# A chunked delta-rule kernel: each level of the triangular inverse forms D and its transpose from one product, and q S leaves PSUM chunk by chunk

## The chip, the cores and the metric

The kernel runs on 1 core of one Trainium2 chip. The metric is the device time of one execution in microseconds (us). Three runs of the kernel before gave 1337.87, 1337.9 and 1339.18 us, so its median is 1337.9 us. The profiled execution is a run of its own.

## The reference, cut to what matters

A decoder trunk of two layers works on 528 tokens (16 meta tokens and 512 others) of width 1024. Layer 0 mixes tokens with a gated delta rule in 8 heads of dimension 128, layer 1 with a short convolution. A gated ConvFFN and a layer norm follow each. The change lies in the delta rule, which the reference writes like this for each head, chunk by chunk:

```
m = where(strict, einsum("id,jd->ij", k_beta, k) * decay, 0)
a_mat = eye(CHUNK) + m
u = triangular_solve(a_mat, v_beta)
w = triangular_solve(a_mat, k_beta * exp(g))
...
v_new = u_i - w_i @ state
o_i = qg_i @ state + qk_i @ v_new
state = state * exp(gl_i) + kd_i.T @ v_new
```

The rest of the trunk is projections by large weight matrices, a width-3 convolution, gating and layer norms.

## The kernel before, in words

**The large products.** Each float32 operand is split into a high part and a rest (`split`, L88 on ACT and L89 on DVE), and each product is three matmuls (L272, L273, L274). Weights come as strips of 128 x 128 blocks: SP loads a strip (L199), ACT and DVE split it, PE uses it.

**The delta-rule stage** is the `with ExitStack() as gctx` block, L313 to L668. It uses 5 chunks of 106 positions (`NC_`, `CH`). It has these parts for each head `hd`:

- `proj` (L392): the q, k and v projections, 144 matmuls into tiles `ps`, with copies to SBUF by ACT (L410, L411), a convolution on DVE (L415) and a Silu on ACT (L417).
- `gdn_a` (L440): transposes and products of k, v and q (tiles `pk`, `pv`, `pn`, `pp`, `pq`, `psNb`), then the inverse of the unit triangular matrix, then one refinement in higher precision (`pr`, `pz`, `py`, L523 to L545), which leaves `DT`.
- `gdn_b` (L548): the recurrence over the 5 chunks. In a chunk, PE multiplies the state `St` by k (L560, `sa[0]`) and by q (L561, `sb`), DVE forms `rr` (L562), PE multiplies by the inverse (L565, `sa[1]`), ACT forms `vn` (L566), PE forms the update (L569, `sa[2]`) and DVE the new `St` (L573). After the last chunk DVE scales all of `sb` into `oS` (L575), PE forms the part within the chunks (L579, L582), and the output is normalised: DVE adds (L580), ACT squares (L589), DVE and POOL form the factor (L591, L592, L593), DVE scales (L594).
- `gdn_c` (L598): PE transposes `oS` (L604, tile `pot`) and ACT copies it into `h` (L607, L608).
- `gate` (L611): the z projection, 48 matmuls into `psz`, a Silu on ACT (L618). When all is done, `h` is multiplied by `zs` (L665), split into `hh` and `hl` (L667), which hold the input of the z projection until then, and POOL issues a DMA that reloads the residual (L668).

**The inverse before** (L497 to L521) has 7 levels, for blocks of 1, 2, 4 up to 64. After level 0, a level is: PE forms p1 from `N16` and `D16` (L502); ACT copies it to `T16` (L507); PE forms p2 from `DT16` and `T16` (L513); DVE copies p2 into `D16` where the level's mask is set (L514); PE transposes `D16` (L518, tile `pt`); ACT copies it to `DT16` (L519). The five chunks are five matmuls of 106 x 106 in float16 in each step. Each of p1, p2 and pt is a new tile of the same PSUM slot (`gtile`, tag `ga0` for even heads, `ga1` for odd ones, one buffer).

**The order of the work.** The generators of a stage are woven (`weave`, L627): while head `hd` is in `gdn_b`, head `hd+1` does the second part of `gdn_a`, head `hd+2` the first `AH` pieces of it, and head `hd-1` its `gdn_c`, after `CW` empty turns. The program order gives priorities; the framework's scheduler then fixes one order for each engine, and takes later work, a `ps` or `psz` matmul above all, where it expects earlier work not to be ready. So `ps` and `psz` are the filler of this stage. After it the first product of the rest of the kernel is `pd` (`down`, L745).

Of the kernel before, what the change touches and what calls it, by code (L numbers as in the profile page):

```python
# [73 lines left out]
def tile_hybrid_trunk(ctx, tc, xt, par, cst, msk, w_ba, w_qkv, w_z, w_ao, w_bi, w_bo, w_up, w_dn, out):  # L74
# [21 lines left out]
    msk_sb = cpool.tile([P, len(LEVELS), CH], U8, name="msk_sb")  # L96
# [216 lines left out]
    with ExitStack() as gctx:  # L313
# [6 lines left out]
        for l0 in (0, NC_):  # L320
            l1 = min(l0 + NC_, len(LEVELS))
            mskf = gp.tile([P, NC_, CH], F32, name=f"mskf{l0}", tag="B", bufs=2)
            nc.sync.dma_start(mskf[:, : l1 - l0, :], msk[:, l0:l1, :])
            V.tensor_copy(msk_sb[:, l0:l1, :], mskf[:, : l1 - l0, :])
# [115 lines left out]
        def gdn_a(hd, box, qT, kT, vT, PT):  # L440
# [7 lines left out]
            NT, DT = full("NT"), full("DT", 3)  # L448
            kd = gp.tile([CH, NC_, P], F32, name=f"kd{hd}", tag="kd", bufs=3)
# [22 lines left out]
            G.tensor_copy(D16, bcm(ident16[:CH, :CH], NC_))  # L472
            yield 900, 1200
# [20 lines left out]
            V.tensor_scalar(N16, NT, NSC, None, ALU.mult)  # L494
            yield 900, 2200

            for li in range(len(LEVELS)):  # L497
                m_d = bcm(msk_sb[:CH, li, :], NC_)
                p1 = gtile(f"p1{hd}{li}", ch)
                for c in R5:  # L500
                    r_ = D16[:, c, :] if li else ident_dn[:CH, :CH]
                    TE.matmul(p1[:CH, c, :CH], N16[:, c, :], r_, start=True, stop=True)  # L502
                last = li == len(LEVELS) - 1
                if li == 0:
                    V.copy_predicated(D16, m_d, p1[:CH, :NC_, :CH])
                else:
                    S.activation(T16, p1[:CH, :NC_, :CH], AF.Copy, scale=1.0 / NSC)  # L507
                    if li == 1:
                        V.scalar_tensor_tensor(L16, NT, NSC, N16, ALU.mult, ALU.subtract)
                    yield 250, 1500  # L510
                    p2 = gtile(f"p2{hd}{li}", ch)
                    for c in R5:
                        TE.matmul(p2[:CH, c, :CH], DT16[:, c, :], T16[:, c, :], start=True, stop=True)  # L513
                    V.copy_predicated(D16, m_d, p2[:CH, :NC_, :CH])  # L514
                yield 250, 1500
                pt = gtile(f"pt{hd}{li}", ch, F16)
                for c in R5:
                    TE.transpose(pt[:CH, c, :CH], D16[:, c, :], ident16[:CH, :CH])  # L518
                S.activation(DT16, pt[:CH, :NC_, :CH], AF.Copy)  # L519
                if not last:  # L520
                    yield 250, 1500  # L521
# [26 lines left out]
        def gdn_b(hd, box):  # L548
# [7 lines left out]
            sb = gbank(f"sb{hd}", "gc")  # L556
            for c in R5:
                r_ = vb[:, c, :]
                if c > 0:
                    TE.matmul(sa[:CH, 0, :], kTv[:, c, :], St, start=True, stop=True)  # L560
                    TE.matmul(sb[:CH, c - 1, :], qTv[:, c, :], St, start=True, stop=True)  # L561
# [5 lines left out]
                yield 220, 800  # L567
                if c < NC_ - 1:
# [6 lines left out]
            V.tensor_tensor(oS[:, 1:, :], sb[:CH], bc(eg[:, hd, 1:], P), ALU.mult)  # L575
            yield 0, 500
# [4 lines left out]
            ps = gbank(f"po0{hd}", "gc")  # L581
            TE.matmul(ps[:CH, 0, :], PT[:, 0, :], vn[:, 0, :], start=True, stop=True)  # L582
            S.activation(oS[:, 0, :], ps[:CH, 0, :], AF.Copy)
# [56 lines left out]
        AH = 14  # L640
# [420 lines left out]
def _layout(inputs):  # L1061
# [60 lines left out]
```

## Time and the profile before

| what | value |
|---|---|
| median of three runs | 1337.9 us |
| profiled execution: its own time | 1337.09 us |
| profiled execution: span from first to last instruction | 1335.3 us |
| delta-rule stage, first matmul to first `pd` matmul | 4.80 to 379.14 us |
| first `psz` matmul | 289.7 us |
| TensorE instructions in the span (matmuls) | 10675 |
| granted clock, mean | 0.997 |

A line of grouped instructions reads: line, engine, operation, output and input by the program's names, shape, count, then busy time in us and the mean of one in ns, then the time that the engine stood idle just before them and what ended it. A line of the waits reads: engine, what waited, what it waited for, us in total, times, longest. A window's line gives, for each engine, its busy time in that stretch.

### The profile page before, as it was taken

What the parts mean: (1) busy time and instruction counts of PE and PEld (TensorE: products, weight loads), DVE (VectorE), ACT (ScalarE), POOL (GpSimd) and SP (SyncE); (2) the same over time, 40 slices, a digit from 0 to 9 for tenths busy, and PEclk for the clock granted to TensorE, in tenths of its full rate; (3) what the DMA queues carried; (4) which work ended last, traced back from release to release, by engine and by line L of the source; (5) the groups of instructions that cost most, each with busy time, mean ns of one, the idle gap of its engine ahead of it and who ended that gap; (6) DMA issues with size and microseconds to landing.
All of it is one profiled execution on the core that took longest, in us unless ns stands there. A gap on an engine that the chain in (4) does not pass through costs nothing.

```text
span 1335.3 us, 26447 instructions
## 1 busy us (share of the span) xinstructions
PE 1296.1 (97%) x10675; PEld 1250.4 (94%) x10675; DVE 1050.1 (79%) x1922; ACT 783.0 (59%) x1632; POOL 92.0 (7%) x132
## 2 busy tenths in 40 slices
PE   7999999999999999999999999999999999999996
PEld 6899989999899999999999999899998998998996
DVE  6667676776567888969869789899689896986976
ACT  5676767776455846636536467466375563663744
POOL 1322333211110000000000000000000000000000
PEclk9999999999999999999999999999999999999999
DMA  6211111111161142522512412335024342252221
GB/s 200 64 49 33 49 48 36 46 49 33 48 224 54 34 150 70 152 64 88 151 64 85 137 56 88 95 95 163 29 64 126 95 144 78 81 141 71 82 70 64
DMA packets 38394, 115.85 MB, mean 87 GB/s; under 512 B 4224, under 2 KB 7808, under 8 KB 38272
## 3 DMA queue, kind: packets, MB, share of 16 engines
q1 hardware_dynamic: 37632, 112.04, 27.9%
q0 software_dynamic: 640, 2.12, 0.5%
q8 instruction: 83, 1.36, 0.4%
q14 instruction: 39, 0.32, 0.1%
HBM read 112.05 MB, written 2.10 MB: 85 GB/s over the span
## 4 chain that ended last, share of the span: by engine, by line
PE 81%; DVE 9%; ACT 5%; DMA 2%; POOL 2%; issue 1%; SPq 0%; ACTq 0%; POOLq 0%; DVEq 0%
PE pd L273 8%; PE pd L274 8%; PE pd L272 8%; PE px L272 6%; PE px L274 6%; PE px L273 6%; PE pz L272 3%; PE pz L273 3%; PE pz L274 3%; PE pu L273 2%; PE pu L274 2%; PE pu L272 2%; PE ps L274 2%; PE ps L273 2%; PE ps L272 2%; PE pq L272 2%
## 5 line engine op out<-in xcount | busy, mean ns | idle before, releaser
L88 ACT ACTIVATE wh<-raw 128x512 fp32r<-128x512 f32 (+3 forms) x321 | 238.3, 747 | 199.7 <-PE pd L273 86.0
L89 DVE TENSOR_TENSOR wl<-raw,wh 128x512 fp32r<-128x512 f32 (+3 forms) x321 | 265.1, 836 | 62.7 <-ACT wh L88 62.0
L272 PE MATMUL pd<-gh,wh 128*128 128x256 f32 (+3 forms) x704 | 212.8, 305 | 4.3 <-DVE bu L853 3.6
L273 PE MATMUL pd<-gl,wh 128*128 128x256 f32 (+3 forms) x704 | 213.7, 304 | 0.1
L274 PE MATMUL pd<-gh,wl 128*128 128x256 f32 (+3 forms) x704 | 213.1, 303 | 0.0
L272 PEld LDWEIGHTS pd<-gh,wh 128*128 128x128 f32 x704 | 132.0, 189 | 10.9 <-DVE bu L853 3.8
L273 PEld LDWEIGHTS pd<-gl,wh 128*128 128x128 f32 x704 | 133.6, 190 | 6.3 <-DVE gl L89 0.4
L274 PEld LDWEIGHTS pd<-gh,wl 128*128 128x128 f32 x704 | 133.5, 190 | 5.8
L88 ACT ACTIVATE wh<-s 128x512 fp32r<-128x512 f32 x132 | 83.3, 631 | 81.8 <-PE pd L273 34.9
L272 PE MATMUL ps<-hh,wh 128*128 128x264 f32 x384 | 114.3, 299 | 0.9 <-ACT acc L411 0.9
L274 PE MATMUL ps<-hh,wl 128*128 128x264 f32 x384 | 114.8, 299 | 0.0
L273 PE MATMUL ps<-hl,wh 128*128 128x264 f32 x384 | 113.9, 297 | 0.0
L273 PE MATMUL pu<-hl,wh 128*128 128x258 f32 (+3 forms) x368 | 105.3, 289 | 1.5 <-DVE hl L743 1.4
L272 PE MATMUL pu<-hh,wh 128*128 128x258 f32 (+3 forms) x368 | 103.9, 288 | 0.4 <-ACT hh L741 0.4
L274 PE MATMUL pu<-hh,wl 128*128 128x258 f32 (+3 forms) x368 | 104.3, 288 | 0.0
L89 DVE TENSOR_TENSOR wl<-s,wh 128x512 fp32r<-128x512 f32 x132 | 90.8, 688 | 14.7 <-ACT wh L88 12.7
L274 PE MATMUL px<-sumh,wl 128*128 128x258 f32 (+1 forms) x352 | 99.7, 283 | 0.0
L272 PE MATMUL px<-hh,wh 128*128 128x258 f32 (+1 forms) x352 | 99.5, 283 | 0.0
L273 PE MATMUL px<-suml,wh 128*128 128x258 f32 (+1 forms) x352 | 99.5, 283 | 0.0
L272 PE MATMUL px<-sumh,wh 128*128 128x258 f32 (+1 forms) x352 | 99.4, 282 | 0.0
L274 PE MATMUL px<-hh,wl 128*128 128x258 f32 (+1 forms) x352 | 99.2, 282 | 0.0
L273 PE MATMUL px<-hl,wh 128*128 128x258 f32 (+1 forms) x352 | 99.1, 281 | 0.0
(298 smaller groups left out, 3814.0 us busy)
## 6 DMA issues: line engine op xcount, KB each, us to landing
raw<-in_w_up_dram SPq DMA_DIRECT2D x88, 512.0 KB, 3.7
raw<-in_w_dn_dram SPq DMA_DIRECT2D x48, 384.0 KB, 3.5
raw<-in_w_bi_dram SPq DMA_DIRECT2D x24, 512.0 KB, 3.8
raw<-in_w_qkv_dram SPq DMA_DIRECT2D x23, 512.0 KB, 3.7
raw<-in_w_z_dram SPq DMA_DIRECT2D x8, 512.0 KB, 3.7
raw<-in_w_ao_dram SPq DMA_DIRECT2D x8, 512.0 KB, 3.6
raw<-in_w_dn_dram SPq DMA_DIRECT2D x16, 256.0 KB, 2.6
raw<-in_w_bo_dram SPq DMA_DIRECT2D x8, 384.0 KB, 3.4
```

Source lines behind the costliest of these rows:

```text
L88: S.activation(hi, src, AF.Copy)
L89: V.tensor_tensor(lo, src, hi.bitcast(F32), ALU.subtract)
L272: TE.matmul(ps, hi[:, k, :], r_h, start=start and k == 0, stop=False, **kw)
L273: TE.matmul(ps, hi[:, k, :], r_l, start=False, stop=False, **kw)
L274: TE.matmul(ps, lo[:, k, :], r_h, start=False, stop=stop and k == nk - 1, **kw)
```

## The change

The inverse of a head keeps one PSUM tile `lv` for all of its levels, and shares a tile `gx` with the other parity. A mask `mskd_sb` now holds a level's mask plus the identity, and `N16` has the scaled identity added, so that the masked product T is the level's block plus the identity, and D times T is the new D in full. With T on DVE, PE forms `DT16 T` (the new D) and `T DT16` (its transpose) in one go, and ACT copies them out with three instructions. `pt` and its transposes go, and so does the masked copy on DVE. `DT16` is prepared by POOL and a masked copy from `NT`.

In the recurrence q S goes to `sa[3]`, in the tile that also takes the other products of the chunk, and ACT copies it with its scale into `oS` for each chunk. The tile `sb`, its scaling at the end and the late product for chunk 0 go; chunk 0's output is written at its own time. `oS` still has one buffer. `AH` becomes 11.

```
+        msk_sb = gp.tile([P, 1 + len(LEVELS), CH], U8, ...)
+        mskd_sb = gp.tile([P, len(LEVELS) - 1, CH], F16, ...)
+        V.tensor_scalar(ident_up, ident[:CH, :CH], NSC, None, ALU.mult)
...
+            V.tensor_tensor(mskd_sb[:, m0 - 1 : m1 - 1, :], mskf[...], bcm(ident[:, :CH], m1 - m0), ALU.add)
...
+        gx = pg.tile([P, 4, P], F32, name="gx", tag="gx", bufs=1)
...
+            G.tensor_copy(DT16, bcm(ident16[:CH, :CH], NC_))
-            V.tensor_scalar(N16, NT, NSC, None, ALU.mult)
+            V.scalar_tensor_tensor(N16, NT, NSC, bcm(ident_up, NC_), ALU.mult, ALU.add)
+            V.copy_predicated(DT16, bcm(msk_sb[:CH, len(LEVELS), :], NC_), NT)
...
-                    S.activation(T16, p1[:CH, :NC_, :CH], AF.Copy, scale=1.0 / NSC)
-                    p2 = gtile(f"p2{hd}{li}", ch)
-                    for c in R5:
-                        TE.matmul(p2[:CH, c, :CH], DT16[:, c, :], T16[:, c, :], start=True, stop=True)
-                    V.copy_predicated(D16, m_d, p2[:CH, :NC_, :CH])
-                for c in R5:
-                    TE.transpose(pt[:CH, c, :CH], D16[:, c, :], ident16[:CH, :CH])
-                S.activation(DT16, pt[:CH, :NC_, :CH], AF.Copy)
+                for c in R5:
+                    TE.matmul(lv[:CH, c, :CH], N16[:, c, :], D16[:, c, :], start=True, stop=True)
+                V.tensor_tensor(T16, lv[:CH, :NC_, :CH], bcm(mskd_sb[:CH, li - 1, :], NC_), ALU.mult)
+                for c in R5:
+                    TE.matmul(lv[:CH, c, :CH], DT16[:, c, :], T16[:, c, :], start=True, stop=True)
+                for c in R5:
+                    o_ = lv[:CH, NC_ + c, :CH] if c < 3 else lx[:CH, c - 3, :CH]
+                    TE.matmul(o_, T16[:, c, :], DT16[:, c, :], start=True, stop=True)
+                S.activation(D16, lv[:CH, :NC_, :CH], AF.Copy, scale=1.0 / NSC)
+                S.activation(DT16[:, lo3, :], lv[:CH, NC_:, :CH], AF.Copy, scale=1.0 / NSC)
+                S.activation(DT16[:, hi2, :], lx[:CH, :, :CH], AF.Copy, scale=1.0 / NSC)
...
-                    TE.matmul(sb[:CH, c - 1, :], qTv[:, c, :], St, start=True, stop=True)
+                    TE.matmul(sa[:CH, 3, :], qTv[:, c, :], St, start=True, stop=True)
+                    S.activation(oS[:, c, :], sa[:CH, 3, :], AF.Copy, scale=eg[:, hd, c : c + 1])
...
+                if c == 0:
+                    TE.matmul(sa[:CH, 3, :], PT[:, 0, :], vn[:, 0, :], start=True, stop=True)
+                    S.activation(oS[:, 0, :], sa[:CH, 3, :], AF.Copy)
...
-            V.tensor_tensor(oS[:, 1:, :], sb[:CH], bc(eg[:, hd, 1:], P), ALU.mult)
...
-            ps = gbank(f"po0{hd}", "gc")
-            TE.matmul(ps[:CH, 0, :], PT[:, 0, :], vn[:, 0, :], start=True, stop=True)
-            S.activation(oS[:, 0, :], ps[:CH, 0, :], AF.Copy)
...
-        AH = 14
+        AH = 11
```

In the changed kernel the lines of this stage stand 8 or 9 further down; the recurrence's matmuls L560, L561, L565, L569 become L570, L571, L576, L583, L579 becomes L591, and L604 becomes L613.

The scheduler's order moves with it. First, PE at the end of the stage. Before, this is what stands on PE just ahead of the first `pd` matmul (`psz71` is the second half of the z projection of head 7):

```order
L272 MATMUL psz71_4952<-hh_68,wh0_82 128x258
L273 MATMUL psz71_4952<-hl_69,wh0_82 128x258
L274 MATMUL psz71_4952<-hh_68,wl0_83 128x258
L272 MATMUL pd0_0_0_33_5059<-hh_68,wh0_82 128x262
L273 MATMUL pd0_0_0_33_5059<-hl_69,wh0_82 128x262
L274 MATMUL pd0_0_0_33_5059<-hh_68,wl0_83 128x262
```

There are 90 `psz` matmuls between head 7's transpose `pot7` and this `pd`. At the same place on PE the changed kernel has this (`sa7` is the recurrence of head 7, `po7` its part within the chunks, `pot7` its transpose):

```order
L583 MATMUL sa7_4323<-vn7_4319,kd7_3860 128x128
L273 MATMUL psz71_4830<-hh_68,wl0_82 128x258
L570 MATMUL sa7_4323<-St7_4321,qkv7_1_3640 106x128
L571 MATMUL sa7_4323<-St7_4321,qkv7_0_3638 106x128
L576 MATMUL sa7_4323<-rr7_4322,DT7_3859 106x128
L591 MATMUL po7_4368<-vn7_4319,PT7_3625 106x128 x4
L613 MATMUL pot7_4387<-cst_sb_71,oS7_4320 128x106 x5
L271 MATMUL pd0_0_0_33_4937<-hh_68,wh0_81 128x262
```

The last `psz` matmul of all now stands ahead of the last chunk of head 7's recurrence, and no filler is left between that chunk and `pd`.

Second, the start of a recurrence on PE, for head 6. Before, its first update (`sa6` from `kd6`) stands among the levels of head 7 (`p173` is p1 of head 7's level 3):

```order
L502 LDWEIGHTS N167_3964
L502 MATMUL p173_4263<-D167_3967,N167_3964 106x106
L272 MATMUL psz20_4638<-hh_68,wh0_82 128x260
L273 MATMUL psz20_4638<-hl_69,wh0_82 128x260
L569 MATMUL sa6_4259<-vn6_4255,kd6_3432 128x128
L274 MATMUL psz20_4638<-hh_68,wl0_83 128x260
```

In the changed kernel it stands behind the transpose of head 5 (`pot5`), which itself stands behind all levels of head 7 (`lv7`, the same PSUM slot):

```order
L613 MATMUL pot5_4202<-cst_sb_71,oS5_3840 128x106 x5
L271 MATMUL psz41_4658<-hh_68,wh0_81 128x258
L272 MATMUL psz41_4658<-hl_69,wh0_81 128x258
L273 MATMUL psz41_4658<-hh_68,wl0_82 128x258
L583 MATMUL sa6_4143<-vn6_4139,kd6_3346 128x128
```

So the chunks of a head's recurrence moved from beside the levels of the next head to behind them.

Third, DVE in the last chunks of head 7. Before (`St7` is the state after chunk 3, `rr7` the input of the last chunk, `oS7` the output):

```order
L665 TENSOR_TENSOR h_67<-h_67,zs4_4753 128x518
L573 SCALAR_TENSOR_TENSOR St7_4444<-St7_4444,egl_267,sa7_4446 128x128
L89 TENSOR_TENSOR wl0_83<-raw32_4693,wh0_82 128x1024
L562 SCALAR_TENSOR_TENSOR rr7_4445<-sa7_4446,nbe7_3959,vb7_3963 106x128
L575 TENSOR_TENSOR oS7_4443<-sb7_4447,eg_265 106x512
L580 TENSOR_TENSOR oS7_4443<-po7_4487,oS7_4443 106x512
```

And in the changed kernel on DVE:

```order
L89 TENSOR_TENSOR hl_69<-h_67,hh_68 128x518 x3
L587 SCALAR_TENSOR_TENSOR St7_4321<-St7_4321,egl_273,sa7_4323 128x128
L89 TENSOR_TENSOR hl_69<-h_67,hh_68 128x518 x3
L573 SCALAR_TENSOR_TENSOR rr7_4322<-sa7_4323,nbe7_3857,vb7_3861 106x128
L89 TENSOR_TENSOR wl0_82<-raw35_4745,wh0_81 128x1024
L592 TENSOR_TENSOR oS7_4320<-po7_4368,oS7_4320 106x512
```

The splits of the next stage's input (`hl`), which stood behind the recurrence, now stand between its last steps. From the first `pd` on, the rows of PE are the same in both kernels.

More of the change, by code (lines that the diff above doesn't have):

```diff
@@ L319, in tile_hybrid_trunk @@
         V.tensor_scalar(ident_dn, ident, 1.0 / NSC, None, ALU.mult)
-        for l0 in (0, NC_):
-            l1 = min(l0 + NC_, len(LEVELS))
-            mskf = gp.tile([P, NC_, CH], F32, name=f"mskf{l0}", tag="B", bufs=2)
-            nc.sync.dma_start(mskf[:, : l1 - l0, :], msk[:, l0:l1, :])
-            V.tensor_copy(msk_sb[:, l0:l1, :], mskf[:, : l1 - l0, :])
+        msk_sb = gp.tile([P, 1 + len(LEVELS), CH], U8, name="msk_sb", tag="msk")
+        mskd_sb = gp.tile([P, len(LEVELS) - 1, CH], F16, name="mskd_sb", tag="mskd")
+        ident_up = gp.tile([CH, CH], F32, name="ident_up", tag="idup")
+        V.tensor_scalar(ident_up, ident[:CH, :CH], NSC, None, ALU.mult)
+        for l0 in (0, 4):
+            mskf = gp.tile([P, NC_, CH], F32, name=f"mskf{l0}", tag="B", bufs=2)
+            nc.sync.dma_start(mskf[:, :4, :], msk[:, l0 : l0 + 4, :])
+            V.tensor_copy(msk_sb[:, l0 : l0 + 4, :], mskf[:, :4, :])
+            m0, m1 = max(l0, 1), min(l0 + 4, len(LEVELS))
+            V.tensor_tensor(mskd_sb[:, m0 - 1 : m1 - 1, :], mskf[:, m0 - l0 : m1 - l0, :],
+                            bcm(ident[:, :CH], m1 - m0), ALU.add)
         def gtile(name, ch=0, dt=F32):
             return pg.tile([P, 8 if dt == F32 else 16, P], dt, name=name, tag=f"ga{ch}", bufs=1)
+        gx = pg.tile([P, 4, P], F32, name="gx", tag="gx", bufs=1)
         def gbank(name, tag):
@@ new lines, in gdn_a @@
+            lv = gtile(f"lv{hd}", ch)
+            lx = gx[:, 2 * ch : 2 * ch + 2, :]
+            for c in R5:
+                TE.matmul(lv[:CH, c, :CH], N16[:, c, :], ident_dn[:CH, :CH], start=True, stop=True)
+            V.copy_predicated(D16, bcm(msk_sb[:CH, 0, :], NC_), lv[:CH, :NC_, :CH])
+            V.scalar_tensor_tensor(L16, NT, NSC, N16, ALU.mult, ALU.subtract)
+            yield 250, 1500
+            for li in range(1, len(LEVELS)):
+                for c in R5:
+                    TE.matmul(lv[:CH, c, :CH], N16[:, c, :], D16[:, c, :], start=True, stop=True)
+                V.tensor_tensor(T16, lv[:CH, :NC_, :CH], bcm(mskd_sb[:CH, li - 1, :], NC_), ALU.mult)
@@ L1095, in _layout @@
         msk[:CH, n] = m
+        if n == 0:
+            msk[:CH, len(LEVELS)] = m.T
     return {
```

23 lines of the change are left out of this document (4 added, 19 removed).

## The prediction

> **What bounds the kernel now.** I read the page first: span, busy time of each engine.
>
> ```profile
> span 1335.3 us, 26447 instructions
> PE 1296.1 (97%) x10675; PEld 1250.4 (94%) x10675; DVE 1050.1 (79%) x1922; ACT 783.0 (59%) x1632; POOL 92.0 (7%) x132
> ```
>
> PE is busy 97% of the span and no other engine comes near it. The change touches only the delta-rule stage, so I read that in windows of 20 us.
>
> ```profile
> 300.00:320.00 20.00, 20.00 (x213) 18.84 (x213) 14.29 (x26) 13.37 (x40) 2.20 (x2) 1.00 0.08 28
> 340.00:360.00 20.00, 18.99 (x158) 17.74 (x157) 10.85 (x21) 7.13 (x18) 1.17 (x1) 1.00 0.16 54
> 360.00:380.00 20.00, 17.93 (x149) 17.43 (x148) 8.92 (x16) 11.25 (x29) 3.42 (x5) 1.00 0.30 87
> 380.00:400.00 20.00, 20.00 (x169) 20.00 (x168) 14.88 (x23) 10.23 (x14) 2.32 (x5) 1.00 0.85 310
> ```
>
> The columns after the stretch are its length, then PE, PEld, DVE, ACT and POOL busy, the granted clock, DMA. PE is full in the middle of the stage and again right after it, and it stands idle for 2.07 us between 360 and 380. DVE and ACT have room. What PE waits for in the stage after its start (20 to 379.2 us) is the waits of PE:
>
> ```profile
> PE sa L560 <- DVE St L573: 3.0, 4, 1.0
> PE pot L604 <- DVE oS L594: 2.5, 2, 1.5
> PE sa L569 <- ACT vn L566: 1.6, 2, 1.2
> PE sa L560 <- DVE St L571: 1.4, 3, 0.6
> PE pn L470 <- DVE vb L466: 1.2, 1, 1.2
> PE ps L272 <- ACT acc L411: 0.9, 2, 0.6
> PE py L544 <- DVE DT L540: 0.9, 1, 0.9
> PE pk L456 <- ACT PT L395: 0.6, 1, 0.6
> PE pd L272 <- ACT zs L618: 0.6, 1, 0.6
> PE psc L379 <- DVE gA L367: 0.6, 1, 0.6
> PE pt L518 <- DVE D L505: 0.2, 1, 0.2
> ```
>
> They sum to 13.5 us of 359 us. The steps of the inverse, which are long chains, hardly appear: only `pt`, with 0.2 us. Filler hides them. So the stage costs what PE has to issue, plus a few waits of the recurrence and of `pot`. A shorter chain is worth little here; fewer matmuls, and whether the filler reaches to the end of the stage, are worth something.
>
> **The change part by part.** First the level in two steps. A step on PE is five small matmuls, and the copies around it are these rows:
>
> ```profile
> 251.00 0.41 PE L502 MATMUL p<-D,N 106*106 106x106 f16 x5
> L502 PE MATMUL p<-D,N 106*106 106x106 f16 x240 | 20.1, 210 | 0.1
> L514 DVE CAST_PREDICATED D<-msk_sb,p 106x530 f16<-106x530 uint8 x48 | 34.0, 708 | 9.8 <-PE p L513 9.6
> L519 ACT ACTIVATE DT<-pt 106x530 f16<-106x530 f16 x56 | 34.2, 612 | 27.5 <-PE pt L518 26.8
> ```
>
> One matmul lasts 0.21 us and five in a row 0.41 us, so one more in a row costs (0.41 - 0.21) / 4 = 0.05 us. A head had 35 p1, 30 p2 and 35 transposes, 100 in all. Now it has 5 for level 0 and 15 for each of 6 levels, 95 in all. Eight heads save 40 matmuls: **-2.0 us** on PE. The steps also lie in fewer groups, but the order shows about as many switches between filler and small matmuls as before, and I give that nothing. The chain of a level gets shorter (one PSUM round trip and one ACT copy of 612 ns less), under filler, so nothing comes of it directly. DVE's masked copy (708 ns) is replaced by a product of the same size from PSUM, for which no row stands; I take the same 708 ns. ACT trades two copies of about 612 ns for three, and adds a copy in each chunk; it was busy 13.37 of 20 us in a full window, so a few per cent more do not make it the bound. The new masks at the start put about 1 us more on DVE, while PE works on other products: I take +0.3 us, between 0 and 1.
>
> Second, the end of the stage, where the forecast is decided. Before, 90 `psz` matmuls stand behind the last transpose `pot7`; in the changed order the last `psz` stands ahead of the last chunk. What happens there before is in the chain of waits from 356 us on:
>
> ```profile
> 356.93 0.47 PE sa L569 x2
> ...
> 358.49 0.22 PE sa L560 x2
> 358.71 0.22 PE sb L561 x2
> ...
> 360.03 0.22 PE sa L565 x2
> ...
> 360.84 1.01 PE po L579 x8
> ...
> 361.87 0.70 DVE oS L580
> ...
> 362.65 0.41 ACT sqb L589 x2
> ...
> 364.94 1.18 POOL ro L593
> ...
> 366.14 0.84 DVE oS L594
> ...
> 367.02 0.67 PE pot L604 x5
> ```
>
> From the update of chunk 3 (356.93) to the end of `pot` (367.02 + 0.67 = 367.69) the chain takes 10.76 us. PE's own share of it is 0.47 + 0.22 + 0.22 + 0.22 + 1.01 + 0.67 = 2.81 us, and one `psz` of 0.12 us is left as filler: 2.93 us. The other 10.76 - 2.93 = 7.8 us were filled with `psz`, and now PE has nothing to issue, because `pd` comes behind `pot7` on the queue. In the changed kernel the chain is not shorter: ahead of the last state and of the last `rr` stand three splits `hl` each on DVE, and `rr` now follows ACT's copy of q S.
>
> ```profile
> L583 ACT ACTIVATE oS<-po x8: 271/278/278, 129.9 to 360.9; 106x128 f32<-106x128 f32 x8
> ```
>
> A copy of this size took 278 ns, so I add 0.3 us, and for the splits nothing, since before the same steps also stood behind a `h` product and a `wl` split; 0 to 2 us is the range. New idle time is 7.8 + 0.3 = 8.1 us. Two waits of before go with it, 1.5 us of `pot` and 0.6 us of `pd`: **+6.0 us**. The filler that stood there has not vanished; it went to the middle of the stage, where the order puts it between steps of the recurrences that now come later. That the middle gets no faster by it is a choice: PE was full there, apart from the waits above.
>
> That the copy stands in the chain at all has a ground in the order: in the changed kernel DVE's `rr` waits for ACT, which it did not before. [...]
>
> Third, PE's clock behind that gap. From the last matmul of `po` to `pot` PE will issue nothing for about 5.1 us (361.85 to 367.02 in the chain above). The one place of the trace with such a gap, apart from the start, is this:
>
> ```profile
> 837.75 0.38 PE L272 MATMUL pd<-gh,wh 128*128 128x256 f32 x1 [3.57 <-DVE bu L853]
> 836.00:840.00 4.00, 2.09 (x11) 1.64 (x12) 4.00 (x8) 1.45 (x3) 0.00 (x0) 0.90 0.56 143
> 840.00:844.00 4.00, 4.00 (x25) 4.00 (x25) 3.15 (x8) 1.15 (x2) 0.00 (x0) 0.67 0.35 123
> ```
>
> After 3.57 us without work the granted clock is 0.90 and then 0.67 in windows of 4 us. The second costs 4 x 0.33 = 1.3 us, the first some 0.2 us of the time in which PE worked: **+1.5 us**, from 0 (the clock holds) to 2.2. [...]
>
> Fourth, seven recurrences now begin behind a `pot` and ACT's first copy into the single `oS` buffer. Three to nine `psz` or `ps` of 0.12 us stand between; a 278 ns copy needs a little more than the three. I take +0.3 us in all, between 0 and 2.
>
> The sum: -2.0 + 0.3 + 6.0 + 1.5 + 0.3 = **+6.1 us**. On the profiled execution that is 1337.09 + 6.1 = 1343.2 us. The median of the runs shown stands 0.8 us above that execution (1337.9), so I forecast **1344.0 us**.
>
> **The rivals.** *The middle gets faster* (the other side). The level's chain is shorter and the recurrence no longer runs beside the levels of the next head, so its steps meet fewer long copies on DVE and ACT. Of the 13.5 us of waits, 2.1 are already in my sum, and 11.4 are left. For it: the rows for `sa` alone, 6.0 us, are waits behind other work on DVE and ACT. Against it: the recurrence steps now have less filler between them. If 9 us of the 11.4 go, the result is 1344.0 - 9 = 1335.0 us. It decides from 8.8 us on, since 6.1 + 2.7 have to be won.
>
> *The end costs less.* The clock holds (-1.5) and some 3 us of the waits in the middle go: 1339.5 us, no change that can be told. Against it: the gap is longer than the one at 834 us.
>
> *The copies in the recurrence wait for ACT.* Every chunk's `rr` now stands behind a copy on ACT's queue, and ACT has long splits there:
>
> ```profile
> L88 ACT ACTIVATE wh<-raw 128x1024 fp32r<-128x1024 f32 (+1 forms) x36 | 37.6, 1043 | 12.2 <-PE ps L273 4.8 <-DMA raw<-in_w_qkv_dram 3.9 <-PE psz L273 3.6
> ```
>
> If 8 of the 32 copies stand behind such a split of 1043 ns with no filler over it, that is 8.3 us more, 1352.3 us. For it: 36 splits in 379 us. Against it: the scheduler knows them, and before the same splits stood ahead of `vn` and cost 1.6 us in all.
>
> **How the numbers follow.** Differences within 0.2% (2.7 us) cannot be told from no change for this kernel; that is 1335.2 to 1340.6 us. Chances: the forecast 0.52, the late copies 0.15, the cheaper end 0.20, the faster middle 0.13. So slower 0.67, same 0.20, faster 0.13. The forecast's own bounds are -2.4 (start 0.3, fourth part 0.3, clock 1.5, copy 0.3) and +5.1 (splits 2, start 0.7, clock 0.7, fourth part 1.7), 1341.6 to 1349.1 us. To hold 8 in 10 the range reaches over most of the cheaper end and up to the late copies: 1336 to 1352 us.
>
> **What would show it.** Right, if in the changed profile PE has a stretch of 7 to 10 us in all without work between the last `psz` and the first `pd`, waiting on DVE's `rr`, ACT's `vn` and DVE's `oS`; if the first `pd` matmul starts some 4 to 5 us later than 379.14; if the clock in the 4 us after it is well below 1.00; and if the rest of the trace from `pd` on is as long as before. Wrong, if the waits of PE ahead of the last head sum to under 4 us (the faster middle), or if `sa L576` waits for `rr` by many us in the middle (the late copies), or if the span differs by more than 2 us behind the stage.

## The result and the profile after

The changed kernel takes 1357.0 us (median of 4 runs, 1355.28 to 1358.37); the kernel before took 1338.2 us beside it. The ratio is 1.0139, 95% interval 1.0127 to 1.0151: 18.8 us slower. The forecast was slower by 6.1 us, 1344.0 us, with a range to 1352. The direction was right, the size a third of what came.

The page of the changed kernel, its first lines:

```profile
span 1355.3 us, 26525 instructions
PE 1299.9 (96%) x10635; PEld 1252.2 (92%) x10635; DVE 1060.2 (78%) x1925; ACT 787.9 (58%) x1704; POOL 105.4 (8%) x140
```

PE has 40 matmuls less, as counted, and yet it is busy 3.8 us longer; some of them run at half the clock (0.50 in a row below). The rest of the loss is time in which PE stands. Windows of the stage, and the first 8 us behind it (columns as in the prediction: length, PE, PEld, DVE, ACT, POOL, granted clock, DMA):

```profile
80.00:100.00 20.00, 17.64 (x163) 16.25 (x162) 13.16 (x17) 14.85 (x35) 10.68 (x10) 1.00 0.18 46
140.00:160.00 20.00, 17.30 (x166) 16.47 (x165) 12.07 (x18) 13.52 (x35) 9.13 (x10) 1.00 0.18 54
260.00:280.00 20.00, 18.18 (x172) 16.28 (x172) 15.19 (x28) 12.01 (x46) 8.48 (x7) 1.00 0.10 28
380.00:400.00 20.00, 11.99 (x69) 10.93 (x68) 10.08 (x16) 10.30 (x23) 3.51 (x6) 0.66 0.60 196
391.70:395.70 4.00, 4.00 (x18) 4.00 (x19) 1.69 (x4) 3.26 (x5) 0.60 (x1) 0.50 0.54 174
395.70:399.70 4.00, 4.00 (x32) 4.00 (x31) 3.55 (x3) 2.58 (x5) 0.00 (x0) 0.90 0.84 269
```

PE is busy 12 of 20 us at the end of the stage, with a clock of 0.66, and the first `pd` matmuls run at 0.50. That end was forecast. The first three rows were not: PE stands for 1.8 to 2.7 us in single windows of the middle, where before it stood for 0.1 to 0.4:

```profile
80.00:100.00 20.00, 19.88 (x214) 18.93 (x213) 14.66 (x23) 15.74 (x37) 2.86 (x5) 1.00 0.19 54
140.00:160.00 20.00, 19.58 (x188) 18.71 (x189) 14.26 (x31) 12.61 (x37) 6.99 (x11) 1.00 0.10 38
260.00:280.00 20.00, 19.73 (x210) 18.57 (x211) 15.30 (x29) 13.04 (x38) 3.73 (x4) 1.00 0.04 14
```

The waits of PE in the stage (20 to 392 us) name them:

```profile
PE pot L613 <- DVE oS L603: 6.3, 2, 5.2
PE pp L486 <- DVE NT L480: 5.8, 4, 2.0
PE lv L524 <- DVE T L520: 4.0, 6, 1.0
PE pn L479 <- DVE vb L475: 2.1, 2, 1.2
PE sa L576 <- DVE rr L573: 1.4, 1, 1.4
PE pd L271 <- ACT h L617: 0.9, 1, 0.9
```

The 5.2 us of `pot`, the 1.4 of `sa` and the 0.9 of `pd` are the end. `pp` and `lv` are new, 9.8 us in the middle, where before the rows for `sa` stood with 6.0. The end itself in the chain of waits, from the last recurrence chunk on:

```profile
377.31 1.92 DVE hl L89 x3
379.23 0.28 DVE St L587
379.52 1.24 DVE hl L89 x3
...
381.26 0.36 DVE rr L573
...
381.66 0.48 PE sa L576 x2
382.16 0.38 ACT vn L577
...
382.58 1.83 PE po L591 x8
...
387.50 1.20 POOL ro L602
388.73 0.84 DVE oS L603
...
389.61 1.16 PE pot L613 x5
...
391.70 0.59 PE pd L271
```

The last `psz` begins at 378.9 us, the first `pd` at 391.70. On PE the last chunk begins like this, with the update of chunk 3 and the product of the new state with k:

```profile
378.69 0.43 PE L583 MATMUL sa<-vn,kd 106*128 106x128 f32 x2
379.57 0.47 PE L570 MATMUL sa<-St,qkv 128*106 128x128 f32 x2 [0.32 <-DVE St L587]
```

The splits `hl` cost no more than what stood there before, as the sum had it: from the update to `sa L576` 2.97 us go by (378.69 to 381.66), against 3.10 in the kernel before (356.93 to 360.03). The `sa L576` that waits 1.4 us for `rr` is a part of the chain that had filler over it before and now has none.

What was not in the sum is that `po` takes 1.83 us and `pot` 1.16 us, where the kernel before took 1.01 and 0.67: the clock falls while the chain still runs, at 382.86 us. It reads 0.50 until 396.51 us, 13.65 us in all. Windows of 3.41 us, four of which cover that stretch, show it:

```profile
379.44:382.86 3.42, 1.43 (x8) 1.02 (x9) 3.35 (x6) 2.56 (x6) 2.21 (x5) 1.00 0.96 321
382.86:386.27 3.41, 1.53 (x8) 1.21 (x6) 0.72 (x2) 0.99 (x5) 0.00 (x0) 0.50 0.91 312
386.27:389.69 3.42, 0.08 (x1) 0.09 (x2) 1.17 (x3) 0.62 (x4) 1.19 (x1) 0.50 0.07 26
389.69:393.10 3.41, 2.47 (x11) 2.14 (x12) 1.04 (x4) 1.52 (x4) 0.00 (x0) 0.50 0.02 5
393.10:396.51 3.41, 3.41 (x18) 3.41 (x17) 1.56 (x2) 3.21 (x5) 0.60 (x1) 0.50 0.84 288
396.51:399.92 3.41, 3.41 (x30) 3.41 (x30) 2.80 (x3) 1.96 (x4) 0.00 (x0) 1.00 0.84 245
```

The costs of the steps themselves were as taken. The product with the mask on DVE, for which there was no row, lasts 705 ns (taken: 708); one matmul of the step lasts 211 ns (before: 210), and five in a row 0.41 us as before:

```profile
L520 DVE TENSOR_TENSOR T<-lv,mskd_sb 106x530 f16<-106x530 f32 x48 | 33.9, 705 | 17.3 <-PE lv L519 11.0 <-ACT zs L627 2.5 <-ACT acc L419 2.2
L524 PE MATMUL lv<-T,DT 106*106 106x106 f16 x240 | 20.4, 211 | 4.0 <-DVE T L520 4.0
```

One more thing appears behind the stage. From the first `pd` to the last matmul the trace before took 946.5 us and the new one 953.9, in the same order of instructions. 2.1 us of the 7.4 lie in the first 40 `pd` matmuls (7.06 us instead of 4.92). Most of the rest lies at two waits that were there before, the one for `gh`, the high part of the input of a later `pd`, some 99 us on (0.7 before) and the one for `bu`, a tile that DVE writes, some 458 us on (3.6 before). At each of them the clock is at 0.50 for a while, from 495.50 to 498.91 us and from 853.90 to 860.73 us. The waits of PE in the two places now:

```profile
PE pd L271 <- ACT gh L88: 2.0, 1, 2.0
PE pd L271 <- DVE bu L862: 5.4, 1, 5.4
```

### The profile page after: what moved, and what is told of

Read it like the earlier page. It is cut to its first block, busy times and chain, and to the rows that moved or that the text cites. A ratio compares the mean times of both kernels' runs of the same rounds, so it can differ in the third digit from the quotient of the medians.

```text
span 1355.3 us, 26525 instructions
## 1 busy us (share of the span) xinstructions
PE 1299.9 (96%) x10635; PEld 1252.2 (92%) x10635; DVE 1060.2 (78%) x1925; ACT 787.9 (58%) x1704; POOL 105.4 (8%) x140
## 4 chain that ended last, share of the span: by engine, by line
PE 80%; DVE 9%; ACT 4%; DMA 3%; POOL 2%; issue 1%; SPq 0%; ACTq 0%; DVEq 0%; POOLq 0%
PE pd L271 8%; PE pd L272 8%; PE pd L273 8%; PE px L271 6%; PE px L273 6%; PE px L272 6%; PE pz L271 3%; PE pz L272 3%; PE pz L273 3%; PE ps L272 2%; PE ps L271 2%; PE ps L273 2%; PE pu L272 2%; DVE wl L89 2%; PE pu L273 2%; PE pu L271 2%
## 6 DMA issues: line engine op xcount, KB each, us to landing
raw<-in_w_dn_dram SPq DMA_DIRECT2D x48, 384.0 KB, 3.7
raw<-in_w_bo_dram SPq DMA_DIRECT2D x8, 384.0 KB, 3.3
```

## The experiments

**What they ask.** The middle lost time that the prediction had left out. Theory A: two buffers are held longer than before. `lv` keeps the PSUM slot of its parity through the whole inverse, where before each product took the slot and gave it back. `psE`, the product from which `PT` is made, always takes the slot of the even heads, and `pot` that of its own head, so both wait for a whole inverse; a late `psE` gives a late `PT`, a late `NT` and a wait at `pp`. And `oS` with its one buffer is now written from the first chunk on, so a recurrence begins only when `pot` of the head before is done. Both use up `psz` early. Theory B: the two-step level itself costs the time. Theory C: the copies of q S on ACT come late.

How a change moves the work shows in the order of PE, counted in large matmuls (1584 stand ahead of `pd`): how many of them stand ahead of the first matmul of a step.

| kernel | `psE` of heads 1, 3, 5, 7 | `pot` of head 7 |
|---|---|---|
| before | 381, 633, 886, 1146 | 1494 |
| after | 436, 691, 987, 1267 | 1584 |
| e1: two `oS` | 436, 668, 958, 1247 | 1539 |
| e2: `lv` anew for each step | 370, 569, 879, 1163 | 1571 |
| e3: both | 370, 569, 846, 1161 | 1505 |
| e4: recurrence alone | 381, 643, 888, 1151 | 1572 |
| e6: after, `psE` in its own parity's slot | 268, 565, 891, 1179 | 1584 |
| e9: inverse alone | 475, 704, 973, 1261 | 1584 |
| e10: e4 with two `oS` | 381, 643, 875, 1144 | 1533 |
| e11: e9 with `lv` anew | 380, 641, 892, 1143 | 1521 |
| e12: all holds away | 268, 578, 901, 1161 | 1485 |

All results, with the ratio to the kernel before in the same session (its median lay between 1338.0 and 1338.6 us). The last three columns are from the trace of one run each: the start of the first `pd`, the time of the first 40 `pd` matmuls, and the time from the first `pd` to the last matmul.

| run | median us | ratio, 95% interval | first `pd` | 40 `pd` | `pd` to last matmul |
|---|---|---|---|---|---|
| before | 1338.2 | | 379.1 | 4.92 | 946.5 |
| after | 1357.0 | 1.0139 (1.0127 to 1.0151) | 391.7 | 7.06 | 953.9 |
| e1 | 1342.8 | 1.0027 (1.0011 to 1.0044) | 381.8 | 4.91 | 949.1 |
| e2 | 1340.0 | 1.0018 (1.0007 to 1.0029) | 380.2 | 4.91 | 953.9 |
| e3 | 1337.7 | 0.9994 (0.9985 to 1.0004) | 377.6 | 4.91 | 947.9 |
| e4 | 1348.1 | 1.0071 (1.0056 to 1.0086) | 389.1 | 4.91 | 947.5 |
| e5 | 1357.7 | 1.0144 (1.0129 to 1.0159) | 391.9 | 6.58 | 953.9 |
| e6 | 1354.0 | 1.0117 (1.0104 to 1.0130) | 387.6 | 7.67 | 953.5 |
| e7 | 1352.3 | 1.0105 (1.0092 to 1.0118) | 392.8 | 6.43 | 949.2 |
| e8 | 1337.0 | 0.9994 (0.9986 to 1.0003) | 376.4 | 4.92 | 948.8 |
| e9 | 1347.0 | 1.0068 (1.0054 to 1.0081) | 384.3 | 6.81 | 953.1 |
| e10 | 1341.9 | 1.0030 (1.0020 to 1.0040) | 383.3 | 4.91 | 946.6 |
| e11 | 1340.7 | 1.0019 (1.0010 to 1.0028) | 379.9 | 4.92 | 949.6 |
| e12 | 1334.9 | 0.9983 (0.9972 to 0.9994) | 374.6 | 4.91 | 947.6 |
| e13 | 1345.4 | 1.0057 (1.0042 to 1.0072) | 383.0 | 6.36 | 949.7 |
| e14 | 1345.3 | 1.0056 (1.0040 to 1.0073) | 385.5 | 4.92 | 946.9 |

The last column of e2 comes from its longest run (1345.99 us, the other nine 1338.9 to 1341.3) and need not be typical of it.

**e1, two `oS` buffers.**

```
-            oS = gp.tile([CH, NC_, P], F32, name=f"oS{hd}", tag="oS", bufs=1)
+            oS = gp.tile([CH, NC_, P], F32, name=f"oS{hd}", tag="oS", bufs=2)
```

> The changed kernel with two oS buffers instead of one, nothing else. Theory A (held buffers: the single oS makes each recurrence begin behind the pot of the head before; lv holds its PSUM slot through the whole inverse, which delays psE of the odd heads and pot): the order leaves 45 products psz behind pot7 instead of none, 45 x 0.12 = 5.4 us of the idle end are filled, the slow clock behind it goes (2.1 us) and the wait at pot6 of 1.1 us; the waits at pp, lv and pn (11.9 us) stay. 1357 - 8.5 = 1348 to 1349 us. Theory B (the two-step level itself is slower, whatever the buffers): the end gets the same gain, since it is the same oS; also 1348 to 1349, so this run sizes the end and does not tell A from B. Rival C (the loss is not filler but late copies on ACT in each chunk): 1355 to 1358 us, the waits only move to sa.

Measured 1342.8 us: 14.2 us of the 18.8 are gone, with one number changed. The size is rough: its five runs reach from 1338.8 us (mean granted clock 0.997) to 1344.4 (0.993), and the traced one (0.994) has 3.41 us of half clock in the middle, from 89.96 us on. Its waits of PE in the stage:

```profile
PE lv L524 <- DVE T L520: 5.7, 5, 1.3
PE pot L613 <- DVE oS L603: 2.6, 2, 1.5
PE pn L479 <- DVE vb L475: 2.6, 3, 1.2
PE pp L486 <- DVE NT L480: 2.1, 2, 1.7
```

The idle end is gone (`pot` 2.6 instead of 6.3), the first 40 `pd` are back at 4.91, and the waits at `lv` stay. The gain is more than the 8 to 9 us expected: `pp` fell as well (5.8 to 2.1), and the trace behind `pd` is 4.8 us shorter. Theory C falls, which had 1355 us or more and the waits at `sa`; these are 1.2 us in all.

**e2, `lv` allocated anew for each step of a level.**

```
             for li in range(1, len(LEVELS)):
+                lv = gtile(f"lv{hd}{li}", ch)
                 for c in R5:
                     TE.matmul(lv[:CH, c, :CH], N16[:, c, :], D16[:, c, :], start=True, stop=True)
...
+                lv = gtile(f"lx{hd}{li}", ch)
                 for c in R5:
                     TE.matmul(lv[:CH, c, :CH], DT16[:, c, :], T16[:, c, :], start=True, stop=True)
```

> The changed kernel in which lv is allocated anew for each step of a level, so that the slot comes free between two steps; oS stays single. Theory A: psE of the odd heads comes in time (filler position 370, 569, 879, 1163 in the order, where it was 436, 691, 987, 1267), so the waits at pp go (5.8 us) and most of those at lv and pn (6.1 us, say 3); pot7 gets 13 products behind it, 1.6 us of the end; 1357 - 10 = 1347 us. Theory B (the level itself): the waits at lv and pp stay, 1355 to 1358 us.

Measured 1340.0 us, 17.0 less. Its waits in the stage (the second product of a level is named `lx` here):

```profile
PE lx L526 <- DVE T L521: 2.8, 4, 1.0
PE pot L615 <- DVE oS L605: 2.4, 2, 1.3
```

`pp` isn't among its waits any more. The tile holds no more data than before and the instructions are the same; only the slot comes free between two steps. Theory B can't stand beside this. The gain is again larger than expected (17.0 instead of 10) and than the sum of the waits named, since the idle end went with it: its last 13 `psz` lie behind `pot`, and the rest lie between the steps of the last head.

**e3, both.** The edits of e1 and e2 together.

> Both: lv anew for each step and two oS buffers. Theory A: 79 products psz stand behind pot7 (90 in the kernel before), so the end has no idle stretch and no slow clock, and the first pd starts at 376 to 380 us; 2 us fewer small products remain as the gain: 1335 to 1340 us. Theory B: the end is repaired but 10 us of waits in the middle stay: 1346 to 1349 us.

Measured 1337.7 us, the same as the kernel before (0.9985 to 1.0004). So the two holds and what follows from them account for the 18.8 us, but for about 1 us: e3 is 0.8 us faster than the kernel before, where 40 matmuls less should give 2.0. The gains of e1 and e2 don't add up (14.2 and 17.0, together 19.3): each of them alone gives `psz` back to the end.

**e4, the recurrence alone** in the kernel before: q S into `sa[3]`, copied by ACT for each chunk into the single `oS`; the old inverse.

```
-                    TE.matmul(sb[:CH, c - 1, :], qTv[:, c, :], St, start=True, stop=True)
+                    TE.matmul(sa[:CH, 3, :], qTv[:, c, :], St, start=True, stop=True)
+                    S.activation(oS[:, c, :], sa[:CH, 3, :], AF.Copy, scale=eg[:, hd, c : c + 1])
...
-            V.tensor_tensor(oS[:, 1:, :], sb[:CH], bc(eg[:, hd, 1:], P), ALU.mult)
```

> The kernel before with only the second half of the change: q S chunk by chunk into sa[3], copied by ACT into the single oS; the old inverse. Theory A: the single oS alone moves pot7 to filler position 1572 of 1584 (1494 in the kernel before); 12 products are left for an end of 8 us, so 6 us idle and 2 us of slow clock, less 2 us of waits that lay there: 1338 + 6 = 1344 us. Theory B (all the loss is in the inverse): 1338 us. Rival C (late copies): over 1346 us with waits at sa spread over the heads.

Measured 1348.1 us, 9.6 over the kernel before; expected 6. The place was wrong too. The end has no idle stretch (40 `pd` in 4.91 us): its few `psz` were enough. The loss lies in the middle, among these waits of PE:

```profile
PE pn L470 <- DVE vb L466: 3.7, 3, 2.3
PE pot L602 <- DVE D L514: 3.2, 3, 1.1
```

`pot` waits for DVE's `D`: a level of another head has its slot. All waits together are only 4.1 us longer than in the kernel before (17.6 against 13.5), and the first `pd` comes 10.0 us later. Stops too short for the list don't fill the rest: all idle pieces of PE together sum to 18.3 us against 14.1. A stretch at half clock in this trace (mean 0.995), 145.32 to 148.74 us, costs an estimated 1.6 us (half of the 3.11 us in which PE was busy). Some 4 us are left, and they lie where PE goes from a large matmul to a small one: from the start of the one to the start of the other, waits taken off, 42.8 us go by in 240 such changes, against 37.9 us in 229 before (counted from 20 us to the first `pd`). The time lies in the range given to rival C, but the sign named for it is missing: the waits at `sa` sum to 2.4 us, not more than the 6.0 of before.

**e10, the recurrence alone with two `oS` buffers.**

> The second half of the change alone, as in e4 (old inverse, q S chunk by chunk), but with two oS buffers. e4 took 1348.1 us. Theory A (all that e4 lost comes from the single buffer, which holds each recurrence back until pot of the head before is done): 51 products stand behind pot7 instead of 12, the waits at pot for the slot of a level go, 1338 to 1340 us. Theory B (the copy in each chunk and the order of its bank cost PE time in the middle): it stays above 1343 us.

Measured 1341.9 us, 3.9 over the kernel before: 5.7 of the 9.6 us are the single buffer. The 3.9 us stay, with the interval clear of 1.000, so theory A is not all. `pn` waits more (4.8 us in 5 waits), and the changes from large to small matmuls take 43.0 us here too (244 of them); what of that is the chunk copies was not taken apart.

**e9, the inverse alone**, with the old recurrence. Since its bank for q S is needed then, two of the five transposed products are formed after `D16` has been copied:

```
-                for c in R5:
-                    o_ = lv[:CH, NC_ + c, :CH] if c < 3 else lx[:CH, c - 3, :CH]
-                    TE.matmul(o_, T16[:, c, :], DT16[:, c, :], start=True, stop=True)
+                for c in range(3):
+                    TE.matmul(lv[:CH, NC_ + c, :CH], T16[:, c, :], DT16[:, c, :], start=True, stop=True)
                 S.activation(D16, lv[:CH, :NC_, :CH], AF.Copy, scale=1.0 / NSC)
+                for c in range(3, NC_):
+                    TE.matmul(lv[:CH, c - 3, :CH], T16[:, c, :], DT16[:, c, :], start=True, stop=True)
```

> The first half of the change alone: the level in two steps with lv held, beside the old recurrence (q S in a bank of its own, copied at the end). Since that bank is then taken, the last two transposed products of a step are written into lv after D16 has been copied out of it, which makes a level one round trip longer. Theory A (the held slot delays psE of the odd heads and pot, and the filler is used up too early): psE of heads 1, 3, 5, 7 stands at filler position 475, 704, 973, 1261 in the order (381, 633, 886, 1146 in the kernel before) and nothing stands behind pot7, so the waits at pp and the idle end with its slow clock come without the single oS: 10 us of idle end less 2 us for fewer small products, some 5 us of waits at pp and lv, 2 us of clock: 1350 to 1354 us. Theory B (the recurrence with the single oS brings the loss): 1337 to 1340 us.

Measured 1347.0 us, 9.0 over the kernel before: between the two theories, outside the range of each and nearer to A. The idle end is there without the single `oS`:

```profile
PE pot L614 <- DVE oS L604: 5.7, 2, 4.5
PE py L554 <- DVE DT L550: 2.7, 2, 1.6
PE pp L485 <- DVE NT L479: 2.1, 3, 1.7
```

The waits at `pp` are 2.1 us, not the 5 expected. Each half of the change alone thus costs 9 to 10 us, and together they cost 18.8.

**e11, the inverse alone with `lv` anew for each step.**

> e9 with lv allocated anew for each step of a level, so that the slot comes free between steps; the old recurrence. Theory A: psE stands at filler position 380, 641, 892, 1143 again and 63 products behind pot7; the gain of 40 fewer small products (2 us) and one copy less in the chain are left: 1335 to 1338 us. Theory B (the step itself costs, whatever is held): within 3 us of e9.

Measured 1340.7 us: 6.4 of the 9.0 us are the held slot. The 2.7 us that stay are more than theory A has. The longer level of this variant is in them, and in the traced run (mean granted clock 0.993) a stretch at half clock from 253.40 us on, 3.41 us long.

**e6, `psE` in the slot of its own parity**, all else as in the changed kernel.

```
-            ps = outer(gA[:, hd, :], gA_hi[:, hd, :], gA_lo[:, hd, :], tri, f"E{hd}", 0, G)
+            ps = outer(gA[:, hd, :], gA_hi[:, hd, :], gA_lo[:, hd, :], tri, f"E{hd}", hd % 2, G)
```

> The changed kernel in which psE of an odd head takes the slot of the odd heads, not that of the even ones; lv is still held through the inverse, oS is single. Theory A (psE behind the held lv makes PT and so NT late, and pp waits for it): the waits at pp go from 5.8 us to under 1 us. The order still leaves nothing behind pot7 (filler position 1584 of 1584), so the idle end of 10 us and the slow clock stay: 1350 to 1353 us. Theory B (the waits at pp come from the level itself): they stay, 1356 to 1358 us. If the time falls below 1346 us, the end was not what I take it for.

Measured 1354.0 us, 3.0 less than the changed kernel and 1 us above the expected range. The waits at `pp` are gone from the list, the end stays:

```profile
PE pot L613 <- DVE oS L603: 6.7, 2, 5.7
PE lv L524 <- DVE T L520: 4.5, 6, 1.1
```

This shows the way from the held slot by `psE` to `pp`, and that the idle end has its own ground in the order, not in `pp`.

**e5, the changed kernel once more**, unedited.

> The changed kernel once more, for a second trace. From the first pd to the end its first trace took 7.4 us more than the kernel before: 2.1 us in the first 40 pd matmuls (clock), the rest at two places where PE waits for the first products of a new weight block. Theory A (the rest is scatter from run to run, which all kernels have there; pd to the end took 946.5 us in the kernel before and 947.5 to 953.9 in the first four experiments): the 40 pd matmuls take 7.1 us again, the gaps behind them come out otherwise, 1354 to 1358 us. Theory B (a lasting effect of the late stage end): the same two gaps of 2.3 and 5.7 us again, 1357 us.

Measured 1357.7 us, and the trace repeats: 40 `pd` in 6.58 us, the wait for `gh` 2.3 us, that for `bu` 5.8. It is not a chance of the first trace.

**e7, work for PE in the idle end.** 13 products more behind `po7`, whose output nothing reads (26 matmuls in the trace).

```
             V.tensor_tensor(oS[:, 1:, :], ps[:CH], oS[:, 1:, :], ALU.add)
+            if hd == NH - 1:
+                ke = gtile("keep", 0)
+                for _ in range(13):
+                    TE.matmul(ke[:CH, 0, :], PT[:, NC_ - 1, :], vn[:, NC_ - 1, :], start=True, stop=True)
```

> The changed kernel with 13 more matmuls between po7 and pot7, copies of the last product of po into a slot that nothing reads: they fill most of the 5.2 us in which PE waits for oS, and lengthen no chain. Theory A (the granted clock falls behind idle time): pot7 starts within 0.5 us of where it did, its five transposes last 0.67 us instead of 1.15, the first 40 pd matmuls take 4.9 us instead of 7.06; 2.6 us less, 1354 us. Theory B (the slow start of pd has another cause, such as the weights' arrival): the 40 pd take 7 us again, 1357 us or more.

Measured 1352.3 us, 4.7 less. But not by the way expected: the 40 `pd` still take 6.43 us. The added products begin at 385.83 us at full clock; the clock fell at 386.30 while they ran, came back at 389.72, and fell again at 393.13, just behind the first `pd` (392.82):

```profile
384.50:386.00 1.50, 1.13 (x10) 1.14 (x11) 0.68 (x1) 0.32 (x1) 0.00 (x0) 1.00 0.91 298
386.00:387.50 1.50, 1.50 (x11) 1.50 (x10) 0.69 (x1) 0.66 (x4) 0.00 (x0) 0.60 0.78 273
...
390.50:392.00 1.50, 0.68 (x5) 0.48 (x5) 0.65 (x1) 0.09 (x1) 0.00 (x0) 1.00 0.03 11
...
393.50:395.00 1.50, 1.50 (x9) 1.50 (x9) 0.94 (x2) 1.45 (x2) 0.00 (x0) 0.50 0.13 22
```

`pot` takes 0.68 us again, and from the update of chunk 3 to the first `pd` it is 11.8 us instead of 13.0. Yet the first `pd` comes 1.1 us later than in the changed kernel, because the stage was 2.3 us late by then: this trace has two stretches of half clock in its middle (157.61 to 161.02 and 266.84 to 270.25 us), and the changed kernel's trace, with the same order on PE up to `po7`, has none there. The gain in total lies behind the stage: the wait for `gh` is 1.3 us and that for `bu` 4.2. Why these became shorter e7 doesn't say.

**e8, `rr` ahead of the copy of q S**, in the kernel of e3.

```
-                    S.activation(oS[:, c, :], sa[:CH, 3, :], AF.Copy, scale=eg[:, hd, c : c + 1])
                     V.scalar_tensor_tensor(rr, sa[:CH, 0, :], nbe[:, c : c + 1], vb[:, c, :], ALU.mult, ALU.add)
+                    S.activation(oS[:, c, :], sa[:CH, 3, :], AF.Copy, scale=eg[:, hd, c : c + 1])
```

> The kernel of e3 (lv anew for each step, two oS buffers) with the order of two instructions turned: DVE's rr ahead of ACT's copy of q S, so that rr does not wait for the copy (278 ns in each of 32 chunks). Theory A (these chains are covered by filler except at the end of a stage that still has 65 products behind pot7): no change from e3, 1337 to 1338 us. Theory B (each chunk costs its copy on PE): 32 x 0.28 = 9 us less, 1329 us; half of it if half is covered, 1333 us.

Measured 1337.0 us, e3's time within the interval: the copy in front of `rr` costs nothing that can be told where filler covers the chunks.

**e12, every hold taken away**: e8 with `psE` in its own parity's slot and `AH = 9`.

> The changed kernel with every hold taken away that the runs showed: lv anew for each step, two oS buffers, psE of odd heads in the other slot, rr ahead of the copy of q S, and the next head started 9 instead of 11 steps ahead; 99 products stand behind pot7 (90 in the kernel before). Theory A (nothing in the stage is held back any more; PE's own work is 2 us less than before, and what is left of waits is the start and pn, lv of single steps): 1334 to 1337 us. Theory B (each further release only moves the waits): 1337 to 1339 us, as e3 and e8.

Measured 1334.9 us, 0.9983 of the kernel before (0.9972 to 0.9994), 3.1 us faster: the version that beats both. No wait of its stage is above 2.2 us in total. The first `pd` starts 4.6 us earlier than in the kernel before; an estimated 2.0 us of that are the 40 matmuls. What `psE` and `AH` bring each was not taken apart, and no run varies `AH` alone.

**e13, an idle end and nothing else**, in the kernel of e3: 14 copies of `oS` onto itself on POOL, which nothing needs.

```
             V.tensor_tensor(oS, oS, bc(ro, P), ALU.mult)
+            if hd == NH - 1:
+                for _ in range(14):
+                    G.tensor_copy(oS, oS)
```

> The kernel of e3 (no idle end, 947.9 us from the first pd to the end, 1337.7 us in all) with one thing added: 14 copies of oS onto itself on POOL ahead of pot7, which nothing else needs, so that PE runs out of products psz and waits for pot7 some 5 to 9 us. Theory A (an idle end costs more behind the stage than its slow clock): the first 40 pd matmuls take 6.5 to 7.5 us instead of 4.9, the wait some 99 us behind the first pd grows from 1.2 to over 2.2 us, and pd to the end takes 952 to 954 us. Theory B (only the slow clock follows from it, the rest is chance): the 40 pd slow down in the same way, the wait at 99 us stays at 1.0 to 1.6 us, and pd to the end takes 949 to 951 us.

Measured 1345.4 us. PE waits 7.2 us for `pot`, the 40 `pd` take 6.36 us, and the first window behind the stage reads:

```profile
383.00:387.00 4.00, 4.00 (x21) 4.00 (x22) 2.66 (x5) 3.97 (x7) 1.77 (x4) 0.59 0.97 302
```

But the wait for `gh` is 1.3 us and the time behind the first `pd` 949.7 us, 1.8 more than in e3. That is little more than the slow clock (1.45 us in the 40 `pd`), as theory B had it: an idle end didn't by itself bring the rest.

**e14, the same late end with PE busy in front of `pd`**: e13 with 18 products that nothing reads, ready after nine of the copies.

> e13 with 18 products that nothing reads, issued when 9 of the 14 copies are through; the order then leaves 30 products psz behind pot7, 3.6 us of work right in front of pd. The stage ends as late as in e13 or 1 to 4 us later. Theory A in the form that the idle stretch or slow clock right in front of pd is what counts: the first 40 pd take 4.9 to 5.5 us, the wait at 99 us is 1.0 to 1.6 us, and pd to the end takes 947 to 950 us. Theory A in the form that the late end of the stage counts, whatever PE does: 952 to 954 us, with a wait at 99 us over 2.2 us. Theory B (chance): no relation.

Measured 1345.3 us, with the 40 `pd` at 4.92 us and 946.9 us behind the first `pd`. So a late end didn't bring it either, and an idle stretch of 4.9 us cost nothing behind the stage. In this trace the clock was back at 378.83 us, and PE worked without a stop from 375.0 to 384.0 us, ahead of `pd` (385.48 us).

## Why the prediction was wrong

By its own steps, on the two profiled executions (1357.38 against 1337.09, 20.3 us; the first `pd` 12.6 us later, the time behind it 7.4 us longer):

- **PE's work, -2.0: held.** 40 matmuls less; five in a row last 0.41 us as before. No run shows the gain by itself; e12, 3.1 us faster than the kernel before, has room for it.
- **The start, +0.3: about 1, but not shown to be the masks.** PE's 192nd matmul of `ps` starts at 46.0 us instead of 44.8. In e13 and e14, with the same masks, it starts at 44.5 and 44.6 us, so the start scatters by more than the term.
- **The end, +6.0: the mechanism was right, the size 8.2.** From the end of the last `psz` to the first `pd` there are 12.7 us, of which PE's work at full clock is 2.4 us; 10.3 us are lost, and the 2.1 us of old waits that lay there are to be taken off. Two terms were missing. The clock falls inside the chain, 0.8 us in `po` and 0.5 in `pot`, where the sum had it only behind the chain. And `pd` still waits 0.9 us for ACT's copy of `pot`, a wait that the sum let go. These 2.2 us are the difference. The splits, taken at 0 with a bound of 2, held: 2.97 us against 3.10 for the two steps. The copy ahead of `rr`, taken at 0.3, doesn't show beside them.
- **The clock behind the gap, +1.5: 2.1.** This trace has 0.50 in the first 4 us and 0.90 in the next: from the first `pd` to 396.51 us it is 4.8 us at half, longer than the 3.41 us of the place from which the 1.5 was read. The reading that gave 1.5 was a little short too: in that place PE was busy for 3.29 us at half the clock (839.22 to 842.63 us), which costs an estimated 1.6.
- **"That the middle gets no faster by it is a choice": this is the step that failed.** The sum kept the waits of the middle as they were, and the only rival on it had them shrink. They grew: PE's waits in the stage sum to 25.1 us, of which 8.3 belong to the end (5.2 `pot`, 1.4 and 0.3 `sa`, 0.9 `pd`, 0.5 `po`); 16.8 are left, against 13.5 - 2.1 = 11.4 before, +5.4. The old ones at `sa` went nearly all, as that rival had it, but `pp` and `lv` came and `pn` grew, because a slot that had been given back at each step is now held for a whole inverse. The text on record says that the steps of the inverse "hardly appear" among the waits and draws from it that only matmuls and filler count. That holds for the length of the chain. It says nothing about what others wait for while the chain holds a buffer. e2, e6 and e9 show it. This term, put at nothing, is 5.4 us before the end, and through the filler that it uses up it is part of the end.
- **Seven recurrences behind `pot` and the single `oS`, +0.3: far too small.** It was priced as one copy at each beginning. e4 against e10 shows 5.7 us for the single buffer with the old inverse, e1 shows 14.2 in the changed kernel. The late beginning delays all that follows in the head, and uses up `psz`. In the sum below this is inside the end, the middle and what came behind.
- **Behind the stage nothing but the clock: 5.3 us more came** (7.4 - 2.1), at the waits for `gh` and `bu` and in the slow clock behind them. e5 repeats it. The wait for `gh` is long in e6 and e9 too (2.6 and 2.9 us), but also in the profiled run of e2 (2.8), which has no idle end; that for `bu` is long in e1, with a wait of 5.5 us, which has none either. e13 has an idle end without it and e14 a late one without it, one trace each. So neither an idle nor a late end is enough to bring it. Near `gh` ACT's split of a weight strip waits for the strip's transfer, 4.9 us in three such waits in the changed kernel against 3.3 us in three before. Why it comes late in these runs, and in both traces of the changed kernel, stays open.

The sum with the measured terms: -2.0 + 1 + 8.2 + 5.4 = 12.6 us ahead of `pd`, as measured, and 2.1 + 5.3 = 7.4 behind it.

Of the signs that the text on record names, two came: PE's waits from the last `psz` to the first `pd` sum to 8.3 us, and the clock behind them is 0.50. Two did not: the first `pd` comes 12.6 us later and not 4 to 5, and the trace behind it is 5.3 us longer than the clock explains.

Of the rivals, the late copies on ACT can be excluded as the cause of the 18.8 us. PE waits for `rr` once in the whole stage, in the end, and there `rr` starts at 381.26 us when DVE's splits are through, while ACT's copy had ended at 380.69. e8, which turns the order, is as fast as e3. What the copies cost in e10's 3.9 us stays open. In the chain ACT's copy starts at 376.39 us and lasts 0.37, and DVE's `rr` follows at 376.90. In seven of the 32 chunks DVE stood idle until that copy was through, 6.2 us in all. What this order costs, 0.3 us in the sum, comes out as nothing that can be told.

## What to carry to other kernels

When a change keeps one buffer over several steps that before took and gave it back step by step, ask for each buffer who else allocates from its slot, and how long those now wait; the wait appears at a consumer far away (here `psE`, then `PT`, `NT`, and PE at `pp`). In a stage whose waits are hidden by filler, every such delay also spends filler, so the bill comes twice: at the place, and at the end where none is left. Count in the order how much filler stands behind the last step of the last chain, and price PE's steps in the bare chain behind it, and the first work after it, at the clock that the trace shows there (here 0.50 from 382.86 us on: `pot` took 1.16 us instead of 0.67, the 40 `pd` 7.06 instead of 4.92).

## What the runs showed of the hardware that was not expected

The clock fell without a long unbroken gap. In the changed kernel it fell at 382.86 us, after pieces of idle time of 0.32, 1.40 and 0.46 us with matmuls in between. In e7 it returned to 1.00 at 389.72 us, after 3.42 us at half in which PE worked without a stop, and was at 0.50 again 3.41 us later, at 393.13 us, when PE had been idle for only 0.71 and 0.94 us in two places with `pot` between them.

The rows of the changed kernel above give PE's busy share beside the clock. It was 1.43 / 3.42 = 0.42 in the window ahead of the fall; in the four windows at half it was 0.45, 0.02, 0.72 and 1.00, and behind the last of them, at 396.51 us, the clock was at 1.00 again. Between 20 and 1300 us this trace has two more stretches at 0.50, of 3.41 and 6.83 us (those at `gh` and `bu`), and that of the kernel before has one, 3.41 us long (839.22 to 842.63 us). The shares are those of the profile, whose matmul ends are modelled. What decides when the clock falls and when it returns is not shown by these numbers.

Two things stand for this case. The first `pd` matmuls ran at 0.50 for 4.8 us, from 391.70 to 396.51; PE was busy for 0.72 of the window in which they began, 389.69 to 393.10, and for all of the next. And the same order on PE did not bring the same clock: up to `po7` e7 has the order of the changed kernel and lost the clock twice in the middle of the stage (157.61 to 161.02 and 266.84 to 270.25 us), while the changed kernel's trace reads 1.00 from 20 us to 382.8 us.
